# The values' projection of a hybrid encoder layer: one written order for all engines, and two of four sums on VectorE

## The chip, the cores and the metric

The kernel runs on one core of a Trainium2 chip. The time is that of the device for one execution of the whole layer, in microseconds (us); the median of several runs counts. The engines of the core are TensorE (PE in the profile, its weight loads PEld), VectorE (DVE), ScalarE (ACT), GpSimd (POOL) and SyncE (SP), which here only issues transfers.

## The reference

One encoder layer over 512 tokens of 1024 channels: a layer norm, a mixer (2-D neighbourhood attention with 16 heads of 64 beside a bidirectional state-space branch, merged by gates), a projection, a layer norm, a squared-ReLU MLP and a last layer norm. What matters here is the mixer's combined input projection and the place of the values in it:

```python
proj = u @ w_in
q, k, v, z, xbc, dt_raw, gate = jnp.split(proj, offs, axis=-1)
ya = neighbourhood_attention(q.reshape(hs), k.reshape(hs), v.reshape(hs), rpb) @ w_attn_br
```

The values `v` are 512 tokens by 1024 columns, from 1024 channels.

## The kernel before, in words

All matmuls are in float32, made of two rounded parts. A tensor is split into a high part (a ScalarE copy to the rounded type) and a low part (a VectorE subtraction, source minus high part). `mm3` multiplies high by high, low by high and high by low, in three matmuls that add into one PSUM bank. `hTh` and `hTl` are the two parts of the normed input, channels on the partitions.

The first half of the layer, the state-space branch, is recorded as a plan and issued in an order that a table of numbers sets; its last work is `ssd_branch(7)`, whose eight accumulators `ps_sbr7_0` to `_7` go through two PSUM banks and are added on VectorE into `ysacc` (line 1032). GpSimd makes the low parts `wl_sbr7` of its weights (line 442).

Behind it stands `project_values` (from line 1103), and behind that the attention, one pair of heads (`pr`) after another: queries and keys of the pair are projected (`ps_q`, `ps_k`, weights `wqk`), ScalarE and GpSimd make the parts `qs` of the queries, VectorE casts `kh` and GpSimd makes `klz` of the keys, then come the scores `pss` on TensorE, the softmax `sc` on VectorE and ScalarE, the transposes `tp_p` and the product with the values (`vhl`). The small loads `raw` (line 1308) bring the bias table, from which GpSimd makes `bias`.

`project_values` computes the values by Strassen's scheme with seven products instead of eight. The tokens fall into two halves and the channels into two halves (kk), so there are four quarters of the input (`quarter`), and four blocks of the weights of 512 rows by 512 columns. Products 1 and 2 take quarters as they are; the others take sums and differences. The sums of high and low part of the four quarters, `f11`, `f12`, `f21`, `f22` in `v_full`, are made on GpSimd (line 1184); VectorE makes the differences from them (lines 1196, 1211, 1213, 1228); `tokens` copies or splits the operand into `vt_...` (ScalarE, then VectorE on line 1149), `split` splits a weight block into `wh_v...` and `wl_v...` (lines 1126 and 1129). Weight blocks are loaded by SyncE into two staging buffers `ws`; sums of blocks are made by accumulating loads that GpSimd issues (`plus`, line 1121). Each product has 24 matmuls of 128x512 into two banks. The results are added on VectorE (`add`, line 1167) and split into `vhl` (`values`, lines 1174 and 1175). They run in the order 1, 2, 5, 3, 6, 7, 4.

Everything from `project_values` on is ordered by a scheduler that works with its own estimates of times; hand-written dependencies (`behind`) push a few instructions back. Every engine executes its own queue strictly in that order, and waits on semaphores where an operand or a buffer is not ready.

Of the kernel before, what the change touches and what calls it, by code (L numbers as in the profile page):

```python
# [283 lines left out]
def encoder_layer(ctx, tc, x, w_in, w_attn_br, w_ssd_br, w_o, w_ff1, w_ff2, pcols, rows64,  # L284
# [822 lines left out]
    def project_values():  # L1107
# [11 lines left out]
        def plus(t, i, n):  # L1119
            for k in (slice(0, 2), slice(2, 4)):  # L1120
                nc.gpsimd.dma_start(t[:, k], block(i, n)[:, k], accum_op=ALU.add)

        def split(name, t, after=None):
            hi, lo = [wide(wp.tile([P, 2112], F32R, tag=n, name=f"{n}_v{name}"), 4) for n in ("wh", "wl")]
            for k in (slice(0, 2), slice(2, 4)):
# [3 lines left out]
                nc.vector.tensor_tensor(out=lo[:, k], in0=t[:, k], in1=hi[:, k].bitcast(F32),
                                        op=ALU.subtract)  # L1130
# [6 lines left out]
        high, low = {}, {}  # L1137

        def tokens(name, parts):
            t = hbp.tile([P, 2, 4, 256], F32R, tag="vt", bufs=3, name=f"vt_{name}")  # L1140
            for b in range(2):
                d = [t[:, n, :, b * P : (b + 1) * P].rearrange("p k (r j) -> p k r j", r=8)
                     for n in range(2)]
                hi, *rest = [x[:, :, :, b * 16 : b * 16 + 16] for x in parts]
                done = nc.scalar.activation(d[0], hi, AF.Copy)
                if rest:
                    nc.scalar.activation(d[1], rest[0], AF.Copy)
                else:
                    low[name] = nc.vector.tensor_tensor(out=d[1], in0=hi, in1=d[0].bitcast(F32),
                                                        op=ALU.subtract)  # L1150
# [19 lines left out]
        def values(s, half, src, after=None):  # L1170
            for j in range(2):
# [3 lines left out]
                x = nc.vector.tensor_tensor(out=vhl[s][:, 2 * half + j, :, 1:3, :], in0=v4,  # L1175
                                            in1=hi.bitcast(F32), op=ALU.subtract)
                if after is not None:
                    behind(x, after, "the tokens of the product before")
            return done

        f21, f22, f11, f12 = [full[:, n].rearrange("p k (r c) -> p k r c", r=8) for n in range(4)]

        def full_sum(f, i, kk):
            return nc.gpsimd.tensor_tensor(out=f, in0=quarter(hTh, i, kk), in1=quarter(hTl, i, kk),
                                           op=ALU.add)
# [10 lines left out]
        nc.vector.tensor_tensor(out=f22, in0=f22, in1=f21, op=ALU.subtract)
# [5 lines left out]
        b21 = split("21", w21)  # L1202
        w22 = load("22", 1, 1)
        sums = gep.tile([P, 2, 512], F32, tag="gt", bufs=4, name="v_sums")
        for j in range(2):
            nc.scalar.activation(sums[:, j], p1[j], AF.Copy)
        p2 = two("2", "tr", "tr")
        product(p2, t12, b21)
        u1 = split("u1", wsum)
        plus(wsum, 1, 1)  # L1210
        nc.vector.scalar_tensor_tensor(out=f22, in0=f22, scalar=-1.0, in1=f11, op0=ALU.mult,
                                       op1=ALU.subtract)
        nc.vector.scalar_tensor_tensor(out=f12, in0=f22, scalar=-1.0, in1=f12, op0=ALU.mult,
                                       op1=ALU.subtract)
        s4 = tokens("s4", [f12])
        p5 = two("5", "mm", "mm")
        product(p5, s1, u1)
        b22 = split("22", w22)
# [642 lines left out]
```

## Time and profile before

| | us |
|---|---|
| median of 3 runs | 1175.56 |
| lowest and highest | 1174.01, 1177.7 |
| the profiled execution's own time | 1175.09 |
| its span in the profile | 1173.3 |
| TensorE busy | 1157.1 |
| VectorE, ScalarE, GpSimd busy | 777.9, 614.4, 558.6 |
| values' projection, first matmul of `ps_v` to first of `ps_q` | 493.88 to 534.97 |

In rows of the timeline the columns are start and duration in us, engine, line, operation, out<-in, shape and count, and in brackets the idle time of that engine just before and what ended it. A row with x2 or more is merged: its duration runs from the first start to the last end. Durations of neighbours overlap by about 0.1 us on VectorE, since an operation starts while the one before drains. SPq is SyncE's queue.

### The profile page before, as it was taken

The page shows a single profiled execution, that of the slowest core. Times are in us where ns is not written, and L with a number is a line of the kernel's source. Part 1 is how long each engine was busy: PE and PEld are TensorE (multiplying, and loading weights), DVE is VectorE, ACT ScalarE, POOL GpSimd, SP SyncE. Part 2 cuts the span into 40 slices and gives each one's busy share as a digit, 9 for nine tenths or more (in the row PEclk, how much of TensorE's full clock was granted, in tenths as well). Part 3 has the DMA queues.
Part 4 walks back from the last instruction along what each step waited for, and adds up shares of the span by engine and source line. Part 5 has one row for each costly group of instructions (what it writes and reads, how often), then busy time and mean ns, then how long its engine had stood idle before and what let it go on. Part 6 is the DMA issues. An engine that isn't in the chain of part 4 may idle for free.

```text
span 1173.3 us, 17112 instructions
## 1 busy us (share of the span) xinstructions
PE 1157.1 (99%) x6420; PEld 979.9 (84%) x6420; DVE 777.9 (66%) x1387; ACT 614.4 (52%) x1042; POOL 558.6 (48%) x600
## 2 busy tenths in 40 slices
PE   8999999999999999999999999999999999999997
PEld 8988788879888888878888888888988888878886
DVE  7857565666657565496888975556552667488855
ACT  6677582846355463555667773342263555365420
POOL 1178968697888776624567630016055131221000
PEclk9999999999999999999999999999999999999999
DMA  6253334333332442475423313543237987878511
GB/s 220 73 186 107 108 109 126 124 124 124 87 137 90 126 138 74 112 153 149 121 51 90 87 37 108 179 170 117 72 108 199 242 196 189 196 202 224 145 75 54
DMA packets 131586, 153.43 MB, mean 131 GB/s; under 512 B 23088, under 2 KB 101936, under 8 KB 131504
## 3 DMA queue, kind: packets, MB, share of 16 engines
q1 hardware_dynamic: 115696, 112.63, 31.0%
q0 software_dynamic: 15232, 38.80, 14.4%
q8 instruction: 50, 0.82, 0.3%
q10 hardware_dynamic: 576, 0.92, 0.2%
q14 instruction: 32, 0.26, 0.1%
HBM read 150.09 MB, written 2.23 MB: 130 GB/s over the span
## 4 chain that ended last, share of the span: by engine, by line
PE 79%; DMA 6%; DVE 5%; POOL 3%; issue 3%; ACT 2%; SPq 2%; DVEq 0%; POOLq 0%; ACTq 0%
PE ps_f L332 8%; PE ps_f L331 8%; PE ps_f L330 8%; PE ps_x L330 4%; PE ps_x L332 4%; PE ps_x L331 4%; PE ps_abr L1419 4%; PE ps_g L332 2%; PE ps_g L331 2%; PE ps_sbr L330 2%; PE ps_g L330 2%; PE ps_sbr L332 2%; PE ps_sbr L331 2%; PE ps_z L330 2%; PE ps_z L332 2%
## 5 line engine op out<-in xcount | busy, mean ns | idle before, releaser
L715 DVE SCALAR_TENSOR_TENSOR cv<-ps_x,pc,cv 128x511 f32<-128x511 f32 (+1 forms) x128 | 95.5, 747 | 32.1 <-ACT cv L707 29.1
L331 PE MATMUL ps_f<-h1Th,wl_f 128*128 128x512 f32 (+1 forms) x288 | 104.0, 365 | 0.0
L330 PE MATMUL ps_f<-h1Th,wh_f 128*128 128x512 f32 (+1 forms) x288 | 103.6, 365 | 0.0
L332 PE MATMUL ps_f<-h1Tl,wh_f 128*128 128x512 f32 (+1 forms) x288 | 102.0, 365 | 0.0
L1622 DVE TENSOR_TENSOR wl_f<-w2r,wh_f 128x1024 fp32r<-128x1024 f32 x42 | 49.9, 1220 | 64.2 <-ACT wh_f L1621 63.9
L330 PE MATMUL ps_z<-wh_z,hTh 128*128 128x256 f32 x256 | 76.0, 297 | 0.3 <-DVE cv L715 0.2
L1616 POOL DMA_DIRECT2D w2r<-in_w_ff x30 | 36.0, 1412 | 75.0 <-DMA w2r<-in_w_ff 49.5
L332 PE MATMUL ps_z<-wl_z,hTh 128*128 128x256 f32 x256 | 71.5, 279 | 0.0
L331 PE MATMUL ps_z<-wh_z,hTl 128*128 128x256 f32 x256 | 71.4, 279 | 0.0
L331 PE MATMUL ps_f<-wh_f,sql 128*128 128x512 f32 x168 | 65.3, 390 | 0.3 <-DVE sql L1622 0.3
L332 PE MATMUL ps_f<-wl_f,sqh 128*128 128x512 f32 x168 | 65.2, 390 | 0.1
L330 PE MATMUL ps_f<-wh_f,sqh 128*128 128x512 f32 x168 | 64.9, 389 | 0.0
L1621 ACT ACTIVATE wh_f<-w2r 128x1024 fp32r<-128x1024 f32 x42 | 42.6, 1052 | 40.8 <-DMA w2r<-in_w_ff 33.0
L330 PEld LDWEIGHTS ps_f<-h1Th,wh_f 128*128 128x128 f32 x288 | 53.9, 188 | 8.9
L331 PEld LDWEIGHTS ps_f<-h1Th,wl_f 128*128 128x128 f32 x288 | 54.0, 188 | 8.8
L313 DVE TENSOR_TENSOR wl_f<-ws_f,wh_f 128x1024 fp32r<-128x1024 f32 x36 | 47.2, 1348 | 20.2 <-ACT wh_f L312 19.7
L332 PEld LDWEIGHTS ps_f<-h1Tl,wh_f 128*128 128x128 f32 x288 | 52.8, 188 | 8.5
L1032 DVE TENSOR_TENSOR ysacc<-ps_sbr,ysacc 128x512 f32<-128x512 f32 x56 | 38.3, 688 | 32.2 <-PE ps_sbr L332 31.7
L330 PE MATMUL ps_x<-hTh,wh_bc 128*128 128x512 f32 (+1 forms) x144 | 57.2, 397 | 0.0
L330 PE MATMUL ps_sbr<-yTh,wh_sbr 128*128 128x512 f32 x128 | 56.7, 443 | 0.1
L330 PE MATMUL ps_x<-hTh,wh_x 128*128 128x512 f32 (+1 forms) x144 | 55.8, 387 | 0.0
L1465 POOL TENSOR_TENSOR gt<-gt,ysacc 128x512 f32<-128x512 f32 x8 | 11.2, 1412 | 90.2 <-ACT gt L1050 90.2
(383 smaller groups left out, 3798.2 us busy)
## 6 DMA issues: line engine op xcount, KB each, us to landing
ws_f<-in_w_ff SPq DMA_DIRECT2D x20, 1024.0 KB, 8.0
w2r<-in_w_ff POOLq DMA_DIRECT2D x18, 1024.0 KB, 8.3
bc<-acs_d SPq DMA_DIRECT2D x32, 512.0 KB, 4.2
w2r<-in_w_ff POOLq DMA_DIRECT2D x30, 512.0 KB, 8.7
ws_bc<-in_w_in SPq DMA_DIRECT2D x16, 512.0 KB, 5.9
ws_x<-in_w_in SPq DMA_DIRECT2D x8, 1024.0 KB, 7.2
ws_z<-in_w_in SPq DMA_DIRECT2D x8, 1024.0 KB, 6.6
ws_g<-in_w_in SPq DMA_DIRECT2D x8, 1024.0 KB, 5.1
```

Source lines behind the costliest of these rows:

```text
L313: (eng[i] if isinstance(eng, tuple) else eng).tensor_tensor(out=lo[:, k], in0=st[:, k], in1=hi[:, k].bitcast(F32), op=ALU.subtract)
L330: nc.tensor.matmul(o, lh, rh, start=start, stop=False)
L331: nc.tensor.matmul(o, ll, rh, start=False, stop=False)
L332: return nc.tensor.matmul(o, lh, rl, start=False, stop=stop)
L715: op("DVE", 0.75, lambda j=j, o=o, n=n: nc.vector.scalar_tensor_tensor(out=acc()[:, o], in0=ps()[:, n], scalar=tap(j), in1=acc()[:, o], op ...
L1032: op("DVE", 0.69, lambda d=d, ps=ps: nc.vector.tensor_tensor(out=ysacc[:, d, :], in0=ps(), in1=ysacc[:, d, :], op=ALU.add), r=[(ps.name, 0 ...
L1419: ins.append(nc.tensor.matmul(pss[j], u, v, start=k + p == 0, stop=k == KD - 1 and p == 2))
L1465: gy = nc.gpsimd.tensor_tensor(out=g1, in0=g1, in1=ysacc[:, d, :], op=ALU.mult)
L1616: nc.gpsimd.dma_start(t, rows(i, n, c, k), accum_op=ALU.add)
L1621: nc.scalar.activation(hi[:, k], x, AF.Copy)
L1622: low = nc.vector.tensor_tensor(out=lo[:, k], in0=x, in1=hi[:, k].bitcast(F32), op=ALU.subtract)
```

## The change

`project_values` from the first difference on is put under `tc.manual_schedule(engines=None)`: every engine then takes these instructions in the order in which the function writes them, and the function is written anew in that order, with the splitting cut into steps (`high`, `low`, `copy`, `rest`). The manual dependencies between splits go. The sums `f11` and `f12` are made on VectorE. The sums `f22` and `f21` stay on GpSimd, but the first accumulating load now waits for them. The load and split of the first pair's weights `wqk` is moved into that part, behind product 4.

```diff
-        def plus(t, i, n):
-            for k in (slice(0, 2), slice(2, 4)):
-                nc.gpsimd.dma_start(t[:, k], block(i, n)[:, k], accum_op=ALU.add)
+        def plus(t, i, n, after=None):
+            for k in pair:
+                dma = nc.gpsimd.dma_start(t[:, k], block(i, n)[:, k], accum_op=ALU.add)
                 if after is not None:
-                    behind(x, after, "the tokens of the product before")
+                    behind(dma, after, "the second half's tokens")
...
-        full_sum(f22, 1, 1)
-        full_sum(f21, 1, 0)
+        def whole(eng, f, i, kk):
+            return eng.tensor_tensor(out=f, in0=quarter(hTh, i, kk), in1=quarter(hTl, i, kk), op=ALU.add)
+
+        whole(nc.gpsimd, f22, 1, 1)
+        after = whole(nc.gpsimd, f21, 1, 0)
         w11 = load("11", 0, 0)
         wsum = load("sum", 0, 1)
-        plus(wsum, 0, 0)
+        plus(wsum, 0, 0, after)
...
-        nc.vector.tensor_tensor(out=f22, in0=f22, in1=f21, op=ALU.subtract)
-        s1 = tokens("s1", [f22])
-        full_sum(f11, 0, 0)
-        full_sum(f12, 0, 1)
-        p1 = two("1", "so", "so")
-        product(p1, t11, b11)
...
+        with tc.manual_schedule(engines=None):
+            less(f22, f22, f21)
+            b21 = slab("21")
+            high(b21, w21)
+            low(b21, w21)
+            w22 = load("22", 1, 1)
+            p1 = product("1", ("so", "so"), t11, b11)
+            s1 = tokens("s1")
+            copy(s1, 0, f22)
+            whole(nc.vector, f11, 0, 0)
+            whole(nc.vector, f12, 0, 1)
+            rest(s1, f22)
...
+            less(f22, f22, f11, -1.0)
+            less(f12, f22, f12, -1.0)
...
+            p4 = product("4", ("so", "so"), t22, u4)
+            wqk = qk_weights(0)
+            add(c22, c22, p7, -1.0)
+            add(sums, sums, p7)
```

On GpSimd the order around the first accumulating load was, with the numbers of the buffers kept in the names (`v_full` holds the four sums, `ws_vsum` is the staging buffer of weight sums):

```order
L442 TENSOR_TENSOR wl_sbr7_4701<-ws_sbr7_4456,wh_sbr7_4699 128x1024 x2
L1121 DMA ws_vsum_4858<-in_w_in 128x2x512 x2
L1184 TENSOR_TENSOR v_full_4853<-hTh_69,hTl_70 128x1024 x4
L1121 DMA ws_vsum_4858<-in_w_in 128x2x512 x2
L1121 DMA ws_v22_4920<-in_w_in 128x2x512 x2
```

and it is now:

```order
L442 TENSOR_TENSOR wl_sbr7_4701<-ws_sbr7_4456,wh_sbr7_4699 128x1024 x2
L1193 TENSOR_TENSOR v_full_4853<-hTh_69,hTl_70 128x1024 x2
L1121 DMA ws_vsum_4860<-in_w_in 128x2x512 x4
L1121 DMA ws_v22_4891<-in_w_in 128x2x512 x2
L1286 MEMSET klz_5187 128x1024
```

Two of the four sums moved ahead of the loads, and two left this queue.

On VectorE, from the last accumulation of the state-space branch to the low half of the tokens of product 3 (`s4`), it was:

```order
L1032 TENSOR_TENSOR ysacc_71<-ps_sbr7_7_4830,ysacc_71 128x512
L1196 TENSOR_TENSOR v_full_4853<-v_full_4853 128x1024
L1129 TENSOR_TENSOR wl_v21_4915<-ws_v21_4862,wh_v21_4914 128x1024 x2
L1228 TENSOR_TENSOR v_full_4853<-v_full_4853 128x1024
L1149 TENSOR_TENSOR vt_s1_4881<-v_full_4853,vt_s1_4881 128x4x128 x2
L1129 TENSOR_TENSOR wl_vu1_4952<-ws_vsum_4858,wh_vu1_4951 128x1024 x2
L1211 SCALAR_TENSOR_TENSOR v_full_4853<-v_full_4853 128x1024
L1167 SCALAR_TENSOR_TENSOR v_c11_5005<-ps_v2_0_4925,v_sums_4922 128x512
L1167 SCALAR_TENSOR_TENSOR v_c11_5005<-ps_v2_1_4926,v_sums_4922 128x512
L1129 TENSOR_TENSOR wl_v22_4993<-ws_v22_4920,wh_v22_4992 128x1024
L1213 SCALAR_TENSOR_TENSOR v_full_4853<-v_full_4853 128x1024
L1129 TENSOR_TENSOR wl_v22_4993<-ws_v22_4920,wh_v22_4992 128x1024
```

and it is now:

```order
L1032 TENSOR_TENSOR ysacc_71<-ps_sbr7_7_4830,ysacc_71 128x512
L1159 TENSOR_TENSOR v_full_4853<-v_full_4853 128x1024
L1134 TENSOR_TENSOR wl_v21_4886<-ws_v21_4864,wh_v21_4885 128x1024 x2
L1193 TENSOR_TENSOR v_full_4853<-hTh_69,hTl_70 128x1024 x2
L1155 TENSOR_TENSOR vt_s1_4919<-v_full_4853,vt_s1_4919 128x4x128 x2
L1134 TENSOR_TENSOR wl_vu1_4955<-ws_vsum_4860,wh_vu1_4954 128x1024 x2
L1161 SCALAR_TENSOR_TENSOR v_full_4853<-v_full_4853 128x1024 x2
L1134 TENSOR_TENSOR wl_v22_4991<-ws_v22_4891,wh_v22_4990 128x1024 x2
L1155 TENSOR_TENSOR vt_s4_4998<-v_full_4853,vt_s4_4998 128x4x128 x2
```

The two sums (line 1193) came in; the difference of line 1228 and the two additions into `v_c11` moved behind the tokens of product 3. Ahead of the first row shown, the order is the same in both: the two halves of `wl_v11` stand between the first additions into `ysacc`.

On SyncE, at the start of the attention (`ws_qk2` are the weights of the third pair of heads, `raw` rows of the bias table), it was:

```order
L304 DMA ws_qk1_5424<-in_w_in 128x8x128 x2
L304 DMA ws_qk2_5669<-in_w_in 128x8x128
L1308 DMA raw0_5268<-in_rpb_pad 16x8x32 x8
L1308 DMA raw1_5345<-in_rpb_pad 16x8x32 x8
L1308 DMA raw2_5513<-in_rpb_pad 16x8x32 x8
L304 DMA ws_qk2_5669<-in_w_in 128x8x128
L304 DMA ws_qk3_5914<-in_w_in 128x8x128 x2
```

and it is now:

```order
L304 DMA ws_qk1_5427<-in_w_in 128x8x128 x2
L304 DMA ws_qk2_5672<-in_w_in 128x8x128 x2
L1335 DMA raw0_5271<-in_rpb_pad 16x8x32 x8
L1335 DMA raw1_5348<-in_rpb_pad 16x8x32 x8
L1335 DMA raw2_5516<-in_rpb_pad 16x8x32 x8
L304 DMA ws_qk3_5917<-in_w_in 128x8x128 x2
```

The second half of `ws_qk2` is issued ahead of the 24 small loads.

More of the change, by code (lines that the diff above doesn't have):

```diff
@@ L1159, in product @@
                         k == 0, k == 3)
-        def two(name, *tags):
-            return [psx.tile([P, 512], F32, tag=tag, bufs=BANKS[tag], name=f"ps_v{name}_{j}")
-                    for j, tag in enumerate(tags)]
+            return pss
         def add(out, x, pss, sign=1.0):
@@ L1168, in add, with values @@
                                                op0=ALU.mult, op1=ALU.add if sign > 0 else ALU.subtract)
-        def values(s, half, src, after=None):
+        def values(s, half, src):
             for j in range(2):
@@ L1174, in values @@
                 done = nc.scalar.activation(hi, v4, AF.Copy)
[L1175 to L1178, printed above, removed]
-            return done
[L1181 to L1185, printed above, removed]
@@ L1187, in project_values @@
-        full_sum(f22, 1, 1)
-        full_sum(f21, 1, 0)
+                nc.vector.tensor_tensor(out=vhl[s][:, 2 * half + j, :, 1:3, :], in0=v4,
+                                        in1=hi.bitcast(F32), op=ALU.subtract)
+            return done
+        pair = (slice(0, 2), slice(2, 4))
+        f22, f21, f11, f12 = [full[:, n].rearrange("p k (r c) -> p k r c", r=8) for n in range(4)]
+        sums, c11 = [gep.tile([P, 2, 512], F32, tag="gt", bufs=4, name=f"v_{n}") for n in ("sums", "c11")]
@@ L1196, in project_values @@
-        nc.vector.tensor_tensor(out=f22, in0=f22, in1=f21, op=ALU.subtract)
-        s1 = tokens("s1", [f22])
-        full_sum(f11, 0, 0)
-        full_sum(f12, 0, 1)
-        p1 = two("1", "so", "so")
-        product(p1, t11, b11)
[L1202 to L1218, printed above, removed]
@@ L1219, in project_values @@
-        plus(w22, 0, 1)
-        s2 = tokens("s2", [f22])
-        c11 = gep.tile([P, 2, 512], F32, tag="gt", bufs=4, name="v_c11")
-        add(c11, sums, p2)
-        u2 = split("u2", wsum, high["s4"])
-        plus(wsum, 1, 0)
-        p3 = two("3", "cb", "yd")
-        product(p3, s4, b22)
-        values(0, 0, c11, low["s4"])
-        nc.vector.tensor_tensor(out=f21, in0=f11, in1=f21, op=ALU.subtract)
-        s3 = tokens("s3", [f21])
-        u3 = split("u3", w22)
-        p6 = two("6", "so", "so")
@@ L1232, in project_values @@
-        product(p6, s2, u2)
-        t22 = tokens("22", [quarter(x, 1, 1) for x in (hTh, hTl)])
-        u4 = split("u4", wsum)
+        t11, t12 = tokens("11"), tokens("12")
+        b11 = slab("11")
+        high(b11, w11)
+        low(b11, w11)
+        for t, kk in ((t11, 0), (t12, 1)):
+            copy(t, 0, quarter(hTh, 0, kk))
+            copy(t, 1, quarter(hTl, 0, kk))
         c12, c22 = [full[:, n].rearrange("p k c -> p (k c)").rearrange("p (j c) -> p j c", j=2)
                     for n in (0, 3)]
-        add(sums, sums, p6)
@@ L1242, in project_values, with qk_weights @@
+        values(0, 0, c11)
         values(1, 0, c12)
-        p4 = two("4", "so", "so")
-        product(p4, t22, u4)
-        add(c22, c22, p7, -1.0)
-        add(sums, sums, p7)
         values(1, 1, c22)
         add(sums, sums, p4)
-        return values(0, 1, sums)
-    vdone = project_values()
+        return values(0, 1, sums), wqk
+    def qk_weights(pr):
+        return weights([(w_in, 0, OFF_Q + pr * P, P), (w_in, 0, OFF_K + pr * P, P)], KD, 256, f"qk{pr}")
+    vdone, first_wqk = project_values()
@@ L1273, in encoder_layer @@
     for pr in range(NH // 2):
[L1274 removed]
+        wqk = qk_weights(pr) if pr else first_wqk
         psq = psx.tile([P, S], F32, tag="mm", bufs=BANKS["mm"], name=f"ps_q{pr}")
```

98 lines of the change are left out of this document (69 added, 29 removed).

## The prediction

> **What bounds the kernel now.** I read the page's first part, then the idle time of TensorE around the changed tiles (the answer on `ps_v`), then the timelines of the stretch engine by engine, and last its table of windows.
>
> ```profile
> span 1173.3 us, 17112 instructions
> PE 1157.1 (99%) x6420; PEld 979.9 (84%) x6420; DVE 777.9 (66%) x1387; ACT 614.4 (52%) x1042; POOL 558.6 (48%) x600
> ```
>
> TensorE (PE) bounds the kernel: only work that it waits for can shorten it. So the question is how much it waits in the values' projection and right behind it. In the windows the columns are length, busy time of PE, PEld, DVE, ACT and POOL with instruction counts, granted clock, DMA share and GB/s.
>
> ```profile
> 493.88:534.97 41.09, 39.23 (x170) 31.38 (x168) 38.40 (x41) 24.22 (x33) 12.53 (x9) 1.00 0.82 172
> 570.18:573.59 3.41, 2.10 (x16) 1.62 (x16) 2.58 (x6) 1.93 (x7) 2.40 (x4) 1.00 1.07 306
> 573.59:577.01 3.42, 3.42 (x11) 2.83 (x10) 3.42 (x16) 1.10 (x2) 1.31 (x4) 0.50 0.22 30
> ```
>
> The first window is the projection, from its first matmul to the first of `ps_q`. It holds 7 products of 24 matmuls. The pace is seen where nothing is waited for, in products 6, 7 and 4, which take 72 matmuls from 518.65 to 534.97, so 0.227 us each:
>
> ```profile
> 500.00 0.39 PE L331 MATMUL ps_v<-wh_v,vt 128*128 128x512 f32 x1
> 501.44 0.50 PE L332 MATMUL ps_v<-wl_v,vt 128*128 128x512 f32 x1 [1.05 <-DVE wl_v L1129]
> 501.77 0.40 PE L330 MATMUL ps_v<-wh_v,vt 128*128 128x512 f32 x1
> 511.32 0.39 PE L332 MATMUL ps_v<-wl_vu,vt_s 128*128 128x512 f32 x1
> 512.44 1.03 PE L330 MATMUL ps_v<-wh_v,vt_s 128*128 128x512 f32 x2 [0.74 <-ACT vt_s L1145]
> 514.10 0.40 PE L330 MATMUL ps_v<-wh_v,vt_s 128*128 128x512 f32 x1
> 518.65 0.39 PE L330 MATMUL ps_v<-wh_vu,vt_s 128*128 128x512 f32 x1
> 534.97 0.39 PE L330 MATMUL ps_q<-hTh,wh_qk 128*128 128x512 f32 x1
> ```
>
> At that pace 168 matmuls take 38.1 us; the window has 41.09. The 3.0 us between are two stops. From 500.00 to 501.77 stand 2 steps (0.45 us at pace) in 1.77: product 2 waits for the low part of its weights and loses 1.32. From 511.32 to 514.10 stand 5 steps (1.13) in 2.78: product 3 waits for its tokens and loses 1.65. No order of this stretch can win more than 2.97 us, 0.25% of the kernel, in the stretch itself. Then the reason for the first stop:
>
> ```profile
> 488.77 10.38 POOL L1184 TENSOR_TENSOR v_full<-hTh,hTl 128x1024 f32<-128x1024 f32 x4
> 494.08 0.69 DVE L1032 TENSOR_TENSOR ysacc<-ps_sbr,ysacc 128x512 f32<-128x512 f32 x1 [0.67 <-PE ps_sbr L332]
> 494.69 5.56 DVE L1196 TENSOR_TENSOR v_full<-v_full 128x1024 f32<-128x1024 f32 x1
> 500.17 2.35 DVE L1129 TENSOR_TENSOR wl_v<-ws_v,wh_v 128x1024 fp32r<-128x1024 f32 x2
> 502.44 1.21 DVE L1228 TENSOR_TENSOR v_full<-v_full 128x1024 f32<-128x1024 f32 x1
> 503.58 1.28 DVE L1149 TENSOR_TENSOR vt_s<-v_full,vt_s 128x512 fp32r<-128x512 f32 x2
> 504.78 2.35 DVE L1129 TENSOR_TENSOR wl_vu<-ws_vsum,wh_vu 128x1024 fp32r<-128x1024 f32 x2
> 566.04 1.35 POOL L1297 TENSOR_TENSOR klz<-kf,kh 64x512 fp32r<-64x512 f32 x1
> 566.29 2.20 DVE L313 TENSOR_TENSOR wl_qk<-ws_qk,wh_qk 128x1024 fp32r<-128x1024 f32 x1
> ```
>
> ```profile
> L1184 POOL TENSOR_TENSOR v_full<-hTh,hTl x4: 3302/3328/3332, 488.8 to 495.9; 128x1024 f32<-128x1024 f32 x4
> ```
>
> The last row is the answer on the tile `v_full` (shortest, median and longest in ns): the records of the four sums overlap. The subtraction of 494.69 takes 5.56 us where the same shape at 502.44 takes 1.21. It ends at 500.25, 1.1 us after GpSimd's (POOL's) four sums end at 499.15: it stood still while they ran, 4.35 us. At 566.29 the same: the VectorE (DVE) operation ends at 568.49, 1.1 us after GpSimd's operation ends at 567.39. The addition at 494.08, which has one input in PSUM, takes its usual 0.69 beside the sums. So here a VectorE operation with two inputs in SBUF and a GpSimd one take turns. The Trainium skill (SBUF — State Buffer, section "SBUF: two separate sides") states that as an exclusive lock held for a whole instruction; the trace agrees, except that at 494.69 VectorE did not get in between the third and the fourth sum.
>
> **The change, part by part.**
>
> *First, two sums go to VectorE.* `f11` and `f12` (1024 elements each) stand on VectorE behind the low parts of `b21`. The pace there is 1.13 us for 1024 elements (500.17 to 502.44 for two) and 0.60 for 512 (503.58 to 504.78 for two, with strided tokens), so the sums cost 2.3 us of VectorE's queue. They replace a standstill of 4.35. The cheap end is 1.13 each, the dear end GpSimd's record, 3.33 each; I take 1.13, since `vt_s` reads the same strided tokens at the usual rate. With the standstill gone `b21`'s low parts end some 1.3 us before product 2 begins, and its stop of 1.32 goes. **-1.32.**
>
> *Second, the fixed order.* Product 3 waited for ScalarE's tokens `s4`, whose difference stood on VectorE behind the standstill, two `c11` additions and a half of `b22`. By the new order VectorE has, from the start of the `f22` subtraction to the first low half of `s4`, 11 operations of 1.13 and 3 of 0.60, 14.3 us, and the high parts that it reads there are copied a little before it comes to each. TensorE begins product 1 (the window's start, 493.88) 0.8 us ahead of that subtraction (494.69) and needs 16.3 us (72 matmuls) to product 3: it is there 15.5 us after it, so 1.2 us of cover is left. The stop of 1.65 goes, and comes back as far as VectorE is late by more than that. **-1.65.** From product 6 on I find each part of VectorE's work ready 1 us or more ahead, as now. In the window VectorE is busy 38.40 us; less 4.35 and plus 2.3 that is 36.3 in about 39.5.
>
> *Third, the other two sums move ahead of the first accumulating load.* GpSimd ends `wl_sbr` at 481.52 and waits then for a transfer until 487.04; the sums of `f22` and `f21` fill that gap, so the load `wsum` itself is hardly later (they start 2.35 us apart, (10.38 - 3.33) / 3, so they end at about 486.3). But VectorE's half `wl_v11` begins at 484.70 in the trace, under the second sum:
>
> ```profile
> 476.78 4.74 POOL L442 TENSOR_TENSOR wl_sbr<-ws_sbr,wh_sbr 128x1024 fp32r<-128x1024 f32 x2 [2.77 <-ACT wh_sbr L438]
> 487.04 2.63 POOL L1121 DMA_DIRECT2D ws_vsum<-in_w_in  x2 [5.52 <-DMA ws_vsum<-in_w_in]
> 484.70 1.22 DVE L1129 TENSOR_TENSOR wl_v<-ws_v,wh_v 128x1024 fp32r<-128x1024 f32 x1
> 485.83 0.69 DVE L1032 TENSOR_TENSOR ysacc<-ps_sbr,ysacc 128x512 f32<-128x512 f32 x1
> 486.61 0.46 PE L330 MATMUL ps_sbr<-yTh,wh_sbr 128*128 128x512 f32 x1
> 488.30 0.50 PE L330 MATMUL ps_sbr<-yTh,wh_sbr 128*128 128x512 f32 x1
> ```
>
> It will stand until 486.3 and end at 487.4 instead of 485.92. Behind it in VectorE's queue waits the `ysacc` addition of 485.83, which frees a PSUM bank for the `ps_sbr` of 486.61; that begins at 488.0. The next low half and addition follow, and the `ps_sbr` of 488.30 begins at 489.7. All that follows on TensorE is 1.4 us later. Bounds: 0 if VectorE gets in ahead, 2.3 if the first takes its whole record of 3.33 from 481.52 on and the second ends at 487.2. I take the value that the paces give. **+1.4.**
>
> *Fourth, the start of the attention.* The first `qk` weights are loaded in the fixed part, and by the order both halves of `ws_qk2` are now issued ahead of 24 small loads `raw`:
>
> ```profile
> 535.44 12.71 SPq L1308 DMA_DIRECT2D raw<-in_rpb_pad  x24
> 548.21 9.04 SPq L304 DMA_DIRECT2D ws_qk<-in_w_in  x5
> 546.05 0.60 ACT L1292 ACTIVATE kf<-ps_k 128x512 f32<-128x512 f32 x1 [1.43 <-PE ps_k L332]
> 552.25 2.01 ACT L312 ACTIVATE wh_qk<-ws_qk 128x1024 fp32r<-128x1024 f32 x2 [5.60 <-DMA ws_qk<-in_w_in]
> 548.33 0.57 DVE L1296 CAST kh<-kf 64x512 fp32r<-64x512 f32 x1
> 546.84 4.45 POOL L1287 TENSOR_TENSOR qs<-qf,qs 64x128 fp32r<-64x128 f32 x10
> 551.74 0.40 PE L1330 MATMUL pss<-kh,qs 128*128 128x256 f32 x2
> 553.34 2.89 DVE L313 TENSOR_TENSOR wl_qk<-ws_qk,wh_qk 128x1024 fp32r<-128x1024 f32 x2 [4.44 <-ACT wh_qk L312]
> 571.68 0.30 PE L1356 MATMUL tp_p<-cst,sc 128*128 128x128 f32 x1 [0.43 <-DVE sc L1345]
> 572.87 1.28 PE L1356 MATMUL tp_p<-cst,sc 128*128 128x128 f32 x7 [0.88 <-DVE sc L1345]
> ```
>
> ScalarE's wait of 5.60 us goes, and the low parts of `wl_qk2` move from 553.34 to right behind the four casts of `kh`. There they meet GpSimd's ten operations on `qs`, which end at 551.29 now, 0.45 us before the scores `pss` need them. Two VectorE operations of 1.1 us in that row put `qs` back by 2.2. The row of the queries is itself some 1.4 earlier, TensorE 1.6; so TensorE stops there for 2.2 + 0.2 - 0.45, about 1.9 us. Bounds: 0 (the two fall beside it) and 2.4. I take 1.9, since the casts end at 548.9 now, in the middle of that row. **+1.9.** In return the first softmax begins 1.4 us earlier against the clock and TensorE is 0.3 later there, so the stop ahead of `tp_p` (0.43 + 0.88) has 1.7 us of air and goes. **-1.31.** Bounds of that: 0 and 1.31.
>
> The half clock at 573.59 (0.50 for 3.42 us, 1.71 us lost) followed a window with TensorE busy 2.10 of 3.41 us. By that row a stop of 1.9 us at `pss` would bring such a window again; I leave it in the sum, **0**. The Trainium skill (TensorE: Matmul & The Clock Gate, section "What's actually happening") lets the clock fall after a whole idle window of about 3.4 us; by that rule the stop would cost no clock, and the sum would be 1.71 us lower. The trace speaks against it: here 1.31 idle of 3.41 was enough.
>
> *Sum:* -1.32 - 1.65 + 1.4 + 1.9 - 1.31 = -1.0 us. The profiled execution took 1175.09 us (span 1173.3), so 1174.1 for its like; it stands 0.47 below the median of the three runs, 1175.56, and by that median the forecast is **1174.6 us**. A measurement of this kernel tells about 0.3% (3.5 us) from no change: the forecast is no change that can be told.
>
> **The rivals.**
>
> *A. The attention's start only gains.* If the low parts of `wl_qk2` and `qs` do not meet, nothing stops at `pss`, and the stop at `tp_p` goes with the half clock behind it: -1.32 - 1.65 + 1.4 - 1.31 - 1.71 = -4.6, 1171.0 us. For it: ScalarE's 5.60 us of waiting end there, and the chain to `tp_p` runs through VectorE's `wl_qk`. Against: the casts end in the middle of the `qs` row.
>
> *B. VectorE becomes the bound (slower).* If each of the two sums costs VectorE what its record lasts on GpSimd, 3.33, it is 4.4 late against 1.2 us of cover at product 3, and 3.2 us of stop come back: the total is 1175.56 - 1.0 + 3.2 = 1177.8, and 1179.5 with one more window of half clock. It decides from 1.7 us per sum on. Against: `vt_s` at 0.60 per 512 elements.
>
> *C. The wait only moves.* If `f22` and `f21` hold VectorE at `wl_v11` as long as the four held it at 494.69 for two of them, 2.4 us, and product 3 keeps half of its stop, the stretch is even (-1.32 - 0.8 + 2.4 = +0.3) and with +0.6 of the attention the total is 1176.4. For it: VectorE did not get in between two sums. Against: only the second sum is left when `wl_v11` comes.
>
> **How the numbers follow.** The forecast's own case 0.48, A 0.25, B 0.12, C 0.15. Faster by over 0.3% needs less than 1172.0: most of A and a little of the forecast's tail, 0.26. Slower by over 0.3% is above 1179.1: B with the half clock and small tails, 0.09. The rest, 0.65, is the same. The range reaches from a little below A, 1170.6, to B's lower price, 1177.8, with about one in ten beyond each end. The forecast's own case alone spans 1172.7 (no stop at `pss`, the half clock stays) to 1177.3 (the bounds 2.3, 2.4 and 0 of the last three terms).
>
> **What would show it.** Right: in the profile after, the subtraction on `v_full` behind the last `ysacc` lasts 1.2 us; VectorE's first `wl_v` lasts about 2.7 instead of 1.22; `ps_v` begins 1.4 us later against `ps_sbr`'s start and runs 168 matmuls in 38.5 us with no stop; the two sums on VectorE last 1.2 each; `wh_qk` of the third pair waits for no transfer; `pss` waits for `qs`; `tp_p` no longer waits at its first use. Wrong: a stop ahead of product 3 or 7 with VectorE named (B), a first `wl_v` that lasts over 3.5 us (C), or a `pss` without a wait and no half clock (A). Orders of instructions in the later heads change too, since a scheduler sets them; I put nothing on that, and it could move the time by one or two such stops of a microsecond either way.

## The result: slower by 0.8%, and the profile after

| | before | after |
|---|---|---|
| median, us | 1176.06 | 1185.6 |
| lowest to highest | 1174.01 to 1180.46 | 1183.95 to 1189.69 |
| ratio to before, 95% interval | | 1.0083, 1.0057 to 1.0108 |
| the profiled execution's time, its span | 1175.09, 1173.3 | 1183.95, 1182.1 |

The forecast was no change (1174.6 us) and its range ended at 1177.8. The first part of the page after:

```profile
span 1182.1 us, 17111 instructions
PE 1157.5 (98%) x6420; PEld 979.1 (83%) x6420; DVE 779.5 (66%) x1389; ACT 615.7 (52%) x1042; POOL 556.8 (47%) x598
```

TensorE is busy about as long as before (1157.5 us, 1157.1 before), so 8.4 of the 8.8 us by which the span grew are idle time. Where they lie is seen from three marks in each profile: the starts of the last `tp_y` (ahead of all that the change moves), of the last `ps_v` and of the last `ps_abr` (the end of the attention).

| | before | after |
|---|---|---|
| start of the last `tp_y` | 478.3 | 480.3 |
| from there to the last `ps_v` | 56.5 | 58.7 |
| from there to the last `ps_abr` | 205.2 | 210.5 |
| from there to the end | 433.3 | 432.6 |

The first row is not the change: the instructions ahead of that mark are the same, and in the twelve other profiles taken here, whose instructions up to there are the same too, it lies between 479.4 and 482.6. So 2.2 us were lost in the values and 5.3 in the attention. (Two matmuls of the attention, the first of `ps_q0` and the first of `ps_k0`, now stand inside the values' stretch, 0.45 us at 0.227 each; without them it is rather 1.8 and 5.7.) The stretches that answer to those of before, with the same columns:

```profile
497.30:539.50 42.20, 39.37 (x172) 31.95 (x172) 37.80 (x45) 24.52 (x34) 7.29 (x6) 1.00 0.78 169
691.00:694.50 3.50, 1.72 (x14) 1.44 (x13) 3.47 (x7) 2.17 (x9) 3.04 (x5) 0.97 0.27 74
694.50:698.00 3.50, 3.50 (x12) 2.98 (x12) 3.46 (x16) 1.69 (x3) 0.00 (x0) 0.54 0.65 228
```

The first is the projection, 42.20 us where it was 41.09; it holds the two matmuls named above and 0.2 us behind the last of product 4, and without these it is about 41.5. In the second TensorE is busy 1.72 of 3.50 us, and behind it runs a stretch at a granted clock of 0.54: the half clock that stood at 573.59 before is now here, 120 us later. The projection's rows in the timeline:

```profile
483.53 4.77 POOL L1193 TENSOR_TENSOR v_full<-hTh,hTl 128x1024 f32<-128x1024 f32 x2
486.75 2.63 DVE L1134 TENSOR_TENSOR wl_v<-ws_v,wh_v 128x1024 fp32r<-128x1024 f32 x1
490.04 0.50 PE L330 MATMUL ps_sbr<-yTh,wh_sbr 128*128 128x512 f32 x1 [1.21 <-DVE ysacc L1032]
500.04 2.01 ACT L1130 ACTIVATE wh_v<-ws_v 128x1024 fp32r<-128x1024 f32 x2 [8.52 <-DMA ws_v<-in_w_in]
498.16 1.21 DVE L1159 TENSOR_TENSOR v_full<-v_full 128x1024 f32<-128x1024 f32 x1
501.13 2.36 DVE L1134 TENSOR_TENSOR wl_v<-ws_v,wh_v 128x1024 fp32r<-128x1024 f32 x2 [1.76 <-ACT wh_v L1130]
503.41 2.35 DVE L1193 TENSOR_TENSOR v_full<-hTh,hTl 128x1024 f32<-128x1024 f32 x2
514.57 0.50 PE L331 MATMUL ps_v<-wh_v,vt_s 128*128 128x512 f32 x1 [0.51 <-DVE vt_s L1155]
535.09 0.50 PE L330 MATMUL ps_q<-hTh,wh_qk 128*128 128x512 f32 x1 [2.32 <-ACT wh_qk L312]
```

Beside GpSimd's two sums VectorE's first `wl_v` lasts 2.63 us, 1.4 longer than before, and `ps_sbr` waits 1.21 for what stands behind it, as forecast. The subtraction on `v_full` lasts 1.21 instead of 5.56, the two sums on VectorE 2.35 together, and product 2 does not stop. But ScalarE waited 8.52 us for `ws_v` (the weights of product 2), VectorE stood 1.76 us for that, product 3 still stops, and `ps_q` stops for 2.32 us inside product 4. At the attention's start:

```profile
550.55 2.01 ACT L312 ACTIVATE wh_qk<-ws_qk 128x1024 fp32r<-128x1024 f32 x2
549.86 6.35 POOL L1314 TENSOR_TENSOR qs<-qf,qs 64x128 fp32r<-64x128 f32 x10
552.57 2.77 DVE L313 TENSOR_TENSOR wl_qk<-ws_qk,wh_qk 128x1024 fp32r<-128x1024 f32 x2
575.57 1.07 PE L1383 MATMUL tp_p<-cst,sc 128*128 128x128 f32 x7 [0.20 <-DVE sc L1372]
```

ScalarE no longer waits for the third pair's weights; GpSimd's `qs` lasts 6.35 us beside VectorE's `wl_qk` (2.77), 4.45 and 2.89 before; `tp_p` waits 0.20 instead of 0.43 + 0.88. The later heads have stops that were not there before:

```profile
560.11 0.17 DVE L1366 TENSOR_SCALAR mx<-mx 128x4 f32<-128x4 f32 x1
643.55 0.39 PE L1357 MATMUL pss<-kh,qs 128*128 128x256 f32 x1 [0.79 <-POOL qs L1314]
645.15 1.99 ACT L312 ACTIVATE wh_g<-ws_g 128x1024 fp32r<-128x1024 f32 x2
646.25 0.49 PE L330 MATMUL ps_g<-hTh,wh_g 128*128 128x512 f32 x1 [0.26 <-ACT wh_g L312]
647.67 0.50 PE L330 MATMUL ps_q<-hTh,wh_qk 128*128 128x512 f32 x1 [0.93 <-ACT qf L1306]
687.00 5.25 POOL L313 TENSOR_TENSOR wl_abr<-ws_abr,wh_abr 128x1024 fp32r<-128x1024 f32 x2
690.03 2.23 DVE L1366 TENSOR_SCALAR mx<-mx 128x4 f32<-128x4 f32 x1
692.30 0.69 DVE L1388 TENSOR_TENSOR ptl<-tp_p,pth 128x512 fp32r<-128x512 f32 x1
693.05 0.38 PE L1397 MATMUL po<-ptl,vhl 128*128 128x256 f32 x1 [1.78 <-DVE ptl L1388]
710.29 0.36 PE L1396 MATMUL po<-pth,vhl 128*128 128x256 f32 x1 [1.35 <-DVE aT L1410]
```

In the middle of the heads ScalarE takes the gate's weights `wh_g` (1.99 us) ahead of the copy `qf` that frees the bank of the next `ps_q`. Near the end the negation of four maxima, 128x4 elements, lasts 2.23 us on VectorE, until GpSimd's `wl_abr` ends (687.00 + 5.25), where the same instruction took 0.17 at 560.11; behind it stands `ptl`, for which `po` waits.

### The profile page after: what moved, and what is told of

The parts are those of the page before. It is cut to its first block, busy times and chain, and to the rows that moved or that the text cites. A ratio compares the mean times of both kernels' runs of the same rounds, so it can differ in the third digit from the quotient of the medians.

```text
span 1182.1 us, 17111 instructions
## 1 busy us (share of the span) xinstructions
PE 1157.5 (98%) x6420; PEld 979.1 (83%) x6420; DVE 779.5 (66%) x1389; ACT 615.7 (52%) x1042; POOL 556.8 (47%) x598
## 3 DMA queue, kind: packets, MB, share of 16 engines
HBM read 150.09 MB, written 2.23 MB: 129 GB/s over the span
## 4 chain that ended last, share of the span: by engine, by line
PE 75%; DVE 8%; DMA 6%; ACT 4%; POOL 3%; issue 3%; SPq 1%; DVEq 0%; POOLq 0%; ACTq 0%
PE ps_f L332 9%; PE ps_f L330 9%; PE ps_f L331 9%; PE ps_x L330 4%; PE ps_abr L1446 4%; PE ps_x L332 4%; PE ps_x L331 4%; PE ps_z L330 2%; PE ps_z L332 2%; PE ps_z L331 2%; PE ps_sbr L330 2%; PE ps_sbr L332 2%; PE ps_sbr L331 2%; DMA ws_vsum<-in_w_in 2%; DMA ws_x<-in_w_in 1%
```

## The experiments

The theory after the comparison, O: the written part and the moved first weights made the scheduler order the heads anew (705 of the 1088 matmuls from `ps_q0` to the last `ps_abr` stand at another place of TensorE's queue), and that order costs most of the loss. The rival, S: the heads only pass on that the values end late. To tell them apart, the order of the attention was taken from one kernel and given to the other: behind the code of the heads, each instruction is put behind the one ahead of it in a table, engine by engine. That sets the order of a queue and is meant to add no wait. The kernel before with its own order as the table was not run, so this is not shown by itself; the traces do show that the tables set the order: in the profiles of a1, a2, a3 and c3 the 1088 matmuls follow one another, by their names, as in that of before, and in b1's as in that of after.

```diff
+    for a, b in zip(order, order[1:]):
+        tc.add_manual_dep(mine_e[b], mine_e[a].name, mybir.DependencyInfo(
+            mybir.DependencyClass.NoSync, mybir.DependencyReason.DATA), reason="the written order")
```

Ratios are to the kernel before on the same chip. The last four columns are of the profile of each, as in the table above.

| run | values | heads | ratio (95%) | last `tp_y` | to last `ps_v` | to last `ps_abr` | to the end |
|---|---|---|---|---|---|---|---|
| before | before | old | 1 | 478.3 | 56.5 | 205.2 | 433.3 |
| after | after | new | 1.0083 (1.0057 to 1.0108) | 480.3 | 58.7 | 210.5 | 432.6 |
| a1 | after | old | 1.0005 (0.9990 to 1.0019) | 482.3 | 57.0 | 204.0 | 432.9 |
| b1 | before | new | 1.0069 (1.0049 to 1.0089) | 479.6 | 56.5 | 212.2 | 432.7 |
| a2 | after, `ps_q0` later | old | 1.0012 (0.9999 to 1.0026) | 482.6 | 55.8 | 205.6 | 433.7 |
| a3 | a2, sums behind the load | old | 0.9985 (0.9971 to 0.9998) | 479.4 | 53.4 | 206.1 | 433.5 |
| c1 | a3 | new up to head 4, then old | 0.9969 (0.9956 to 0.9983) | 482.5 | 53.5 | 203.0 | 432.3 |
| c3 | before, two sums on VectorE | old | 0.9977 (0.9962 to 0.9993) | 479.8 | 54.4 | 204.3 | 432.3 |
| e1 | c3 | new up to head 4, then old | 0.9979 (0.9968 to 0.9990) | 479.9 | 54.4 | 203.3 | 433.6 |
| c4 | before | old up to head 4, then new | 1.0086 (1.0062 to 1.0110) | 479.7 | 56.2 | 212.8 | 432.3 |
| e2 | before | new from head 5 to about 10 only | 1.0062 (1.0043 to 1.0080) | 480.7 | 56.4 | 214.2 | 432.6 |
| d1 | after | a third order | 1.0053 (1.0034 to 1.0072) | 480.5 | 57.4 | 209.7 | 432.7 |
| f1 | before | new, one swap | 1.0070 (1.0050 to 1.0091) | 479.8 | 56.4 | 213.0 | 432.3 |
| f2 | before | new, `wh_g` later | 1.0069 (1.0047 to 1.0092) | 482.3 | 56.3 | 211.1 | 432.3 |

**a1: the changed kernel with the old order of the heads.** The first pair's weights go back into the loop, and the table is that of the kernel before.

```diff
-            wqk = qk_weights(0)
...
-        wqk = qk_weights(pr) if pr else first_wqk
+        wqk = qk_weights(pr)
...
+    pin(nc.cur_bb.bb.instructions[mark:])
```

> The changed kernel, with the instructions of the attention, from the first pair's weights to the branch projection, in the order that each engine had in the kernel before; the values' part stays as changed. Theory O (the scheduler made another order of the heads, and that order is what costs): the stops of TensorE at the scores, po and the last transposes, 8.7 us in the profile after against 3.9 before, come back to about 4, so the time falls by 4.8 us or somewhat more to 1178 to 1181 us, ratio to the kernel before 1.001 to 1.004; what is left are the stop of 1.4 us at ps_sbr and that of 2.5 us at ps_q0, less the 2.1 us won in products 2 and 3. Theory S (the heads only pass on a late start of the values): the order does not matter, 1184 to 1187 us, ratio 1.007 to 1.010.

Measured: ratio 1.0005, 1178.41 us. Nearly all of the loss is gone, with the values' part as changed. O held, S fell. In its profile the old stops at the first transposes are back, and `ps_q0`, which stands at the same place inside product 4, lost only 0.3 us there, since its weights came sooner:

```profile
534.19 2.01 ACT L357 ACTIVATE wh_qk<-ws_qk 128x1024 fp32r<-128x1024 f32 x2 [1.20 <-DMA ws_qk<-in_w_in]
576.25 0.30 PE L1439 MATMUL tp_p<-cst,sc 128*128 128x128 f32 x1 [0.43 <-DVE sc L1428]
577.43 1.07 PE L1439 MATMUL tp_p<-cst,sc 128*128 128x128 f32 x7 [0.88 <-DVE sc L1428]
```

**b1: the kernel before with the new order of the heads.** The same table the other way round; no line of the values differs.

> The kernel before, with the instructions of the attention in the order that each engine has in the changed kernel; the values' part stays as before. Theory O: the time rises by 4.8 us or somewhat more, 1180.5 to 1183.5 us, ratio 1.004 to 1.007, and the stops of the changed kernel at the scores of head 10, at ps_q7, at po13 and po14 are there. Theory S: within 1 us of the kernel before, ratio 0.999 to 1.001.

Measured: 1.0069, at the upper end of what O expected. TensorE's stops in its profile:

```profile
645.02 0.50 PE L373 MATMUL ps_g<-hTh,wh_g 128*128 128x512 f32 x1 [1.93 <-ACT wh_g L355]
646.44 0.50 PE L373 MATMUL ps_q<-hTh,wh_qk 128*128 128x512 f32 x1 [0.93 <-ACT qf L1334]
691.82 0.39 PE L1425 MATMUL po<-ptl,vhl 128*128 128x256 f32 x1 [1.79 <-DVE ptl L1416]
709.02 0.36 PE L1424 MATMUL po<-pth,vhl 128*128 128x256 f32 x1 [1.35 <-DVE aT L1438]
```

They are those of the changed kernel, and the same engines and tiles end them. (Some of the expectations name other heads for the last two stops; they stand at `po12` and `po15`.) As in the changed kernel, a half clock of 3.41 us begins behind the stop at `po12`, here at 692.21.

**a2: `ps_q0` behind product 4.**

```diff
+            if e == "PE":
+                tc.add_manual_dep(mine_e[order[0]], ends["4"].ins.name, mybir.DependencyInfo(
+                    mybir.DependencyClass.NoSync, mybir.DependencyReason.DATA), reason="behind the last product")
```

> As the run with the old order of the heads, and the first matmul of ps_q0 stands behind the last of product 4 instead of behind its eighth; nothing else moves. If the stop there (2.5 us lost in the profile after, for weights whose transfer is not there yet) is lost for good: 2.2 to 2.5 us less than that run. Rival: the heads behind it wait for the same weights or for the vector engine anyway, and 0 to 0.8 us are won.

Measured: 1.0012 against 1.0005 for a1, so no gain that can be told: the rival held. Two rows of its profile:

```profile
536.20 2.01 ACT L357 ACTIVATE wh_qk<-ws_qk 128x1024 fp32r<-128x1024 f32 x2 [2.32 <-DMA ws_qk<-in_w_in]
574.70 0.39 PE L1458 MATMUL po<-ptl,vhl 128*128 128x256 f32 x1 [1.17 <-DVE ptl L1449]
```

The weights came at 536.20, 8.2 us after their load was issued at 528.04; in a1 it was 534.19 after 527.98 (6.2), in the changed kernel 533.98 after 525.68 (8.3). So the size of the stop at `ps_q` is that of one transfer in one execution. And where TensorE does not wait there, it comes earlier to `po`, which then waits 1.17 for VectorE.

**a3: the two sums on GpSimd behind the first accumulating load again.** As a2, and:

```diff
-        whole(nc.gpsimd, f22, 1, 1)
-        after = whole(nc.gpsimd, f21, 1, 0)
...
-        plus(wsum, 0, 0, after)
+        for f, kk in ((f22, 1), (f21, 0)):
+            x = whole(nc.gpsimd, f, 1, kk)
+            x_prev = plus(wsum, 0, 0) if kk else x_prev
+            tc.add_manual_dep(x.ins, x_prev.ins.name, mybir.DependencyInfo(
+                mybir.DependencyClass.NoSync, mybir.DependencyReason.DATA), reason="behind the first load")
```

> As the run with ps_q0 behind product 4, and GpSimd's two sums f22 and f21 stand behind the first accumulating load again, as in the kernel before; nothing else moves. If the stop at ps_sbr (1.4 us) comes from these sums under VectorE's wl_v11: 1.4 us less, VectorE's first wl_v back at 1.2 us. Rival: the sums meet VectorE a little later (second half of wl_v11, first difference of f22) and 0 to 0.5 us are won. All taken together this kernel would then stand at 1173 to 1176 us, ratio 0.997 to 1.000, since the 2.1 us won in products 2 and 3 stay.

Measured: 0.9985 after a2's 1.0012, some 3 us where 1.4 were expected. The rows:

```profile
485.82 1.22 DVE L1182 TENSOR_TENSOR wl_v<-ws_v,wh_v 128x1024 fp32r<-128x1024 f32 x1
495.25 2.01 ACT L1178 ACTIVATE wh_v<-ws_v 128x1024 fp32r<-128x1024 f32 x2 [4.65 <-PE ps_sbr L377]
496.94 2.36 DVE L1182 TENSOR_TENSOR wl_v<-ws_v,wh_v 128x1024 fp32r<-128x1024 f32 x2
571.64 1.60 PE L1447 MATMUL tp_p<-cst,sc 128*128 128x128 f32 x8 [1.53 <-DVE sc L1436]
```

`wl_v` is back at 1.22; ScalarE's copies of product 2's weights begin at 495.25 and wait for TensorE, not for a transfer; VectorE has no idle time ahead of 496.94; and the stretch from the last `tp_y` to the last `ps_v` is 53.4 us, 2.4 shorter than in a2, with no stop in any of the seven products. The 1.53 at `tp_p` shows what was late next.

**c1: a3, with the first four heads in the new order.** Both orders have the same set of instructions up to one place on each engine (331 matmuls on TensorE); the table is the new one up to there and the old one from there.

> As the run with the sums back behind the first load, and the first four heads take the order that the changed kernel has (second half of ws_qk2 issued ahead of the small loads raw), the later heads keep the old one. In that run TensorE lost 3.5 us at the first transposes: 2.3 us of stops at 568 to 570 us and 1.2 us of half clock behind. In the kernel before with the changed heads 0.3 us was lost at the same place, and 0.5 at the scores before it. Theory O: 2.5 to 3 us less than the run with the sums back, 1172 to 1173 us where the kernel before takes 1177.4, ratio 0.995 to 0.997. Rival (TensorE only comes earlier to later heads, whose chains through ScalarE and VectorE are not earlier): 0 to 0.8 us, ratio 0.998.

Measured: 0.9969, 1173.48 us against 1176.46 for the kernel before. The step from a3, 0.0016, lies between the two expectations, and the intervals overlap. In the profile `tp_p` waits 0.22 and no half clock follows; 1.09 us stand at a later `po`. It is the fastest of all, as fast as c3 within the intervals.

**c4: the kernel before, with only the later heads in the new order.**

> The kernel before, with the first four heads in its own order and the later ones in the order that the changed kernel has. With all heads in the new order it was 1.0069. Theory O with the place named: the early heads in the new order win 2.5 to 3 us, so the later ones alone cost some 10.5 us: ratio 1.008 to 1.0105, 1187 to 1190 us. Rival: the cost is spread over all heads, or an earlier start feeds the later stops, and the later ones alone cost 5 us or less, ratio 1.004 or less.

Measured: 1.0086, some 10 us: the loss sits in the heads behind the fourth. One of its stops brought a half clock with it, in the second of these windows:

```profile
645.00:648.20 3.20, 1.97 (x7) 1.39 (x8) 3.20 (x12) 3.17 (x6) 0.00 (x0) 0.94 0.14 17
648.20:651.60 3.40, 3.40 (x10) 2.68 (x9) 3.31 (x11) 2.65 (x6) 2.58 (x4) 0.56 0.28 93
```

**e2: only the middle heads new.** The table is old, then new for 354 places of TensorE, then old.

> The kernel before, with the heads 5 to about 10 in the order of the changed kernel and all others in the old one. With all later heads in the new order it was 1.0086, some 10 us. In that profile TensorE lost 3.3 us at 643 to 645 us and 1.4 us of half clock behind, and 3.4 us at po14 and po15. Theory: the two places share the cost, and this run shows 4.5 to 6 us, ratio 1.0035 to 1.005. Rivals: the end of the heads carries it all (less than 1.5 us here, ratio under 1.0015), or the middle does (ratio 1.007 or more).

Measured: 1.0062, more than the sharing that was expected and less than "the middle alone". The stops in the middle are there,

```profile
649.66 0.49 PE L374 MATMUL ps_g<-hTh,wh_g 128*128 128x512 f32 x1 [1.95 <-ACT wh_g L356]
651.09 0.50 PE L374 MATMUL ps_q<-hTh,wh_qk 128*128 128x512 f32 x1 [0.93 <-ACT qf L1335]
```

and this run had smaller ones at the end of the heads too, 1.6 us together between 671 and 692. So the middle alone costs most of the loss. That the end has a part too is not shown: the step to c4, 0.0024, lies inside the intervals, and the end alone in the new order was not run. (This profile, of the slowest of its six executions, also has two half clocks of 3.41 us, from 577.19 and from 652.28, behind the first transposes and behind the stops in the middle.)

**c3: only the two sums on VectorE**, in the kernel before.

```diff
-        full_sum(f11, 0, 0)
-        full_sum(f12, 0, 1)
+        full_sum(f11, 0, 0, nc.vector)
+        full_sum(f12, 0, 1, nc.vector)
```

> The kernel before with one edit: the sums f11 and f12 are made on VectorE. No written order; the heads keep their old order. The term of the prediction for this part alone: product 2's stop of 1.3 us goes; product 3's stop of 1.5 us shrinks to about 0.7, since VectorE is 2 us further while TensorE comes 1.3 earlier: 1.3 to 2 us less, ratio 0.998 to 0.999, and the two sums last 1.2 us each. Rival: the standstill of VectorE moves to another subtraction, or a sum on VectorE takes the 3.3 us of its record on GpSimd: ratio 1.000 or above.

Measured: 0.9977. The table holds the old order of the heads here too; whether the scheduler would keep it by itself is not shown. VectorE's sums and subtraction, and what is left of product 3's stop:

```profile
496.23 2.35 DVE L1229 TENSOR_TENSOR v_full<-hTh,hTl 128x1024 f32<-128x1024 f32 x2
498.49 1.22 DVE L1241 TENSOR_TENSOR v_full<-v_full 128x1024 f32<-128x1024 f32 x1
512.99 0.50 PE L376 MATMUL ps_v<-wh_v,vt_s 128*128 128x512 f32 x1 [0.39 <-DVE vt_s L1194]
```

**e1: c3, with the first four heads in the new order.**

> The kernel before with the two sums f11 and f12 on VectorE, no written order in the values, and the first four heads in the order of the changed kernel, the later ones in the old order. The two sums alone gave 0.9977; the early heads gave 0.9985 to 0.9969 in the kernel with the written order. If the two add up: 0.995 to 0.997, 1171 to 1173 us, and the stops of 1.7 us at the first transposes are 0.4 us or less. Rival: the early heads only win where the written order has brought TensorE forward: 0.9970 to 0.9985, no gain over the two sums.

Measured: 0.9979, no gain over the sums alone: the rival held. The stops at the first transposes went (0.35 us left of 1.7) and 1.2 us were lost at a `po` at 624.10 instead of 0.6 in c3.

**d1: the changed kernel with the first weights in the loop, no table.** The scheduler makes a third order. The matmuls between the last transpose of a head and the second matmul of its `po`, at 0.227 us for 512 columns and some 0.1 for the short ones, are the cover for `pth` and `ptl`:

| head | old order | new order | third order |
|---|---|---|---|
| 12 | 5.6 | 7.9 | 7.4 |
| 13 | 7.4 | 5.6 | 4.5 |
| 14 | 6.2 | 2.3 | 1.2 |
| 15 | 2.2 | 0.1 | 0.1 |

> The changed kernel with one line back in its old place: the first pair's weights are loaded in the loop of the heads instead of behind product 4. The scheduler then makes a third order of the heads. By the matmuls that stand between the last transpose and po of a head (at 0.227 us each), heads 14 and 15 have 1.1 and 0 us of cover there, in the changed kernel 2.2 and 0, in the kernel before 6.1 and 2.0. Theory O: as slow as the changed kernel, 1184 to 1188 us, ratio 1.006 to 1.010, with the stops at po14 and po15. Rival (the move of the first weights is what costs): 1177 to 1180 us, ratio 1.000 to 1.003.

Measured: 1.0053, 1183.29 us, a little under what was expected and clear of the rival. Its heads ran at the full clock (granted clock 1.00 from 540 to 745), so the loss needs no half clock. Three of its stops:

```profile
609.36 0.38 PE L1395 MATMUL po<-pth,vhl 128*128 128x256 f32 x1 [0.54 <-ACT pth L1386]
695.86 0.35 PE L1395 MATMUL po<-pth,vhl 128*128 128x256 f32 x1 [1.17 <-DVE aT L1409]
708.29 0.36 PE L1395 MATMUL po<-pth,vhl 128*128 128x256 f32 x1 [1.35 <-DVE aT L1409]
```

The last two name not `pth` or `ptl` but `aT`, as `po15` does in the changed kernel and in b1. The kernel gives `po` one PSUM bank, and VectorE's additions into `aT` are the last to read it. In the changed kernel's profile, between `po14` and `po15`:

```profile
708.58 0.59 ACT L1407 ACTIVATE low<-po 64x512 f32<-64x512 f32 x1 [0.51 <-PE po L1397]
709.21 0.94 DVE L1410 TENSOR_TENSOR aT<-po,low 64x128 f32<-64x128 f32 x5 [0.42 <-ACT low L1407]
```

From the last matmul of `po14`, at 708.21, to the first of `po15`, at 710.29, pass 2.08 us. In the old order 4 transposes and 9 matmuls of 512 columns stand between them, some 2.5 us at the same rates; in the new and the third order only the 4 transposes, some 0.4. For the stop at `po15` this is the cover that counts, and not the one in the table.

**f1 and f2: one stop of the new order at a time.** f1 swaps two neighbours on VectorE, f2 moves the split of `wh_g` behind `qf`. The rows are the names of what the table's numbers stand for, VectorE's and ScalarE's.

```diff
-mx14 ptl12_1
+ptl12_1 mx14
...
-wh_g1_0 wh_g1_0 qf6 pth8_0 kf6 low7
+qf6 pth8_0 kf6 low7 wh_g1_0 wh_g1_0
```

> The kernel before with all heads in the order of the changed kernel (that gave 1.0069), and one swap on VectorE: the low part ptl12_1, for which po12 waited 1.9 us at 691.8, stands ahead of the negation of head 14's maxima (mx, 128x4) instead of behind it. In that run the negation lasted 2.2 us instead of 0.17, until GpSimd's wl_abr had ended. If this standstill is what the stop consists of: the stop at po12 goes and 1.9 us with it, ratio about 1.0053, and the negation still lasts 2 us beside wl_abr. Rival: po12 waits for something else at the same time (its transposes, ScalarE's pth), and the stop stays at 1 us or more.

```profile
691.38 0.69 DVE L1416 TENSOR_TENSOR ptl<-tp_p,pth 128x512 fp32r<-128x512 f32 x1
691.99 1.64 DVE L1394 TENSOR_SCALAR mx<-mx 128x4 f32<-128x4 f32 x1
694.23 1.95 PE L1411 MATMUL tp_p<-cst,sc 128*128 128x128 f32 x8 [0.85 <-DVE sc L1400]
```

Measured: 1.0070. The stop at `po12` is gone, so the standstill was its cause; the negation still lasts 1.64, and now the transposes behind lose 1.4 us (0.85 idle at the first), waiting for the softmax that follows it in VectorE's queue. So the swap takes away 1.9 us at one place and 1.4 come back at the next, and the time did not change. The half clock moved too: this profile has one of 6.83 us from 645.24 on, behind the stop in the middle, where b1's has none, and none at 692.21, where b1's has 3.41 us.

> The kernel before with all heads in the order of the changed kernel (1.0069), and the split of the gate's weights wh_g one place later: on ScalarE behind the four copies that follow it, on VectorE its first low half behind head 10's scores, on TensorE its first matmul behind ps_q7. There TensorE lost 2.1 + 1.2 us at 642.8 to 646.4, waiting for wh_g and then for the copy qf behind it in ScalarE's queue. If the place of wh_g in the queue is what costs: qf follows the exponentials at 643.9, ps_q7 begins at 644.5 and 1.7 us of the 3.3 go, ratio about 1.0055. Rival: wh_g is only late because of its transfer or the exponentials hold everything: 0 to 0.5 us.

```profile
645.87 0.57 ACT L1334 ACTIVATE qf<-ps_q 128x512 f32<-128x512 f32 x1
646.49 0.51 PE L373 MATMUL ps_q<-hTh,wh_qk 128*128 128x512 f32 x1 [1.48 <-ACT qf L1334]
```

Measured: 1.0069. `ps_q7` waits for `qf` alone, 1.48 us of idle time; of the 3.3 us that TensorE lost there 1.6 are left, as expected. The time cannot be told from b1's.

## Why the prediction was wrong, step by step

**The two sums (-1.32): right, and the best of the change.** They last 1.2 us each on VectorE and the standstill of 4.35 us went with product 2's stop. Alone they give 0.9977 (c3), 2.7 us: half of product 3's stop goes with them.

**The written order (-1.65): half right in the changed kernel.** Product 3 still lost 0.67 us there (1.03 in a1, 0.74 in a2). The sentence that failed is that the high parts "are copied a little before it comes to each": the weights of product 2 were late and VectorE stood 1.76 us, more than the 1.2 of cover. With the sums back in place (a3) the whole term is there. Over c3, which has no written order, the order adds nothing that the intervals can tell.

**The two sums ahead of the first load (+1.4): the mechanism was right, the term too small.** The stop at `ps_sbr` lost 1.37 us. But `wl_v11` also frees the staging buffer into which product 2's weights are loaded; I followed only the queue of VectorE behind it, not the transfer that waits for it. With the sums moved, that transfer was issued 10.8 us behind the last `tp_y` in all four profiles, and 9.4 in the ten others. It also took longer from issue to landing, 8.8 to 9.2 us against 5.9 to 8.4; why is not shown. Undoing the move gave back 2.7 thousandths (a2 to a3), some 3 us.

**The start of the attention (+1.9 and -1.31): a miss on one, right on the other.** The casts were followed by `wl_qk` beside `qs` as forecast, and `qs` lasted 1.9 us longer; but TensorE did not wait at `pss` in the changed kernel, and 0.5 us in b1. The stop at `tp_p` went, and the half clock at that place too, as in rival A.

**Product 4 (0).** I wrote that from product 6 on each part of VectorE's work is ready in time, and did not look for instructions of the attention inside the projection: the scheduler had put `ps_q0` and `ps_k0` behind the eighth matmul of product 4. It cost 2.3 us in the one profile; a2 shows no steady price.

**The later heads (0): the step that failed.** I put nothing on the new order there and wrote that it could move the time "by one or two such stops of a microsecond either way". It costs 0.0069 alone (b1, 8 us), and without it the change is within 0.2% of before (a1). It is the place from head 5 on (c4), and most of it the middle heads (e2); what the first four heads win is not clear of the noise (0.0016 from a3 to c1, nothing from c3 to e1). The order was there to be read before the run: the gate's weights ahead of `qf` on ScalarE, a tiny operation and `ptl` behind GpSimd's `wl_abr`, and 0.4 us of cover between `po14` and `po15` where the old order has 2.5, beside chains of ScalarE and VectorE work that the trace before gave durations for. Of the rivals, none named it.

What stays open: the price of each stop in the new order, and how much of the loss belongs to the end of the heads. f1 and f2 each took away the stop that they were meant to, 1.9 and 1.7 us, and the time stayed: in f1 the next instruction waited for most of it, and intervals of 0.004 hide the rest. And why the scheduler chose these orders cannot be read from a trace.

## What to carry to other kernels

Where a scheduler orders what follows, an edit is also a new draw of that order: read the whole new order at the places where the bounding engine has little cover, and price it, or fix the old one and time the edit alone. A wait has to be followed along the buffers as well as along the queue: what the late instruction frees may be the staging buffer of the next transfer. Of a change with several parts, the smallest may hold the gain: two engine names gave 0.9977 here, with the old order of the heads held.
